# A state-space stage on one core: the block-wise complex recurrence becomes a rotation and one real scan per tile, with its DRAM round trips on another queue and a new order

## The chip, the cores and the metric

The program runs on one core of a Trainium2 chip. TensorE (PE) multiplies matrices, VectorE (DVE) and ScalarE (ACT) work on tiles of 128 partitions, GpSimd (POOL) does some element work, and SP, ACT and POOL issue DMAs. The metric is the device time of one execution in microseconds; lower is better. Runs of the kernel before: 2762.75, 2764.63 and 2765.36 us, median 2764.63.

## What is computed

Two attention blocks, then a second model of two layers; its first layer mixes with a diagonal complex state-space recurrence (64 groups of 16 channels, 64 complex states each, 512 steps). Cut to that mixer:

```python
u = (h @ w_in).reshape(bsz, seq, N_GROUPS, SSM_GROUP)
dt = exp(log_dt)[:, None]
mag = exp(a_re * dt)
ab_re, ab_im = mag * cos(a_im * dt), mag * sin(a_im * dt)
...   # bb = input matrix times (ab - 1) / a
bu_re = einsum('blgh,gph->blgp', u, bb_re)
bu_im = einsum('blgh,gph->blgp', u, bb_im)
# s[t] = ab * s[t-1] + bu[t], complex, along the 512 steps
_, _, s_re, s_im = associative_scan(combine, (ab_re, ab_im, bu_re, bu_im), axis=1)
y = einsum(s_re, c_re) - einsum(s_im, c_im) + d_skip * u
z = gelu(y) @ w_glu
return z[..., :D_MODEL] * sigmoid(z[..., D_MODEL:])
```

## The kernel before

The whole program is one plan of items (`Plan`), each a function with the weight units it needs. `run` walks the items and puts weight DMAs (`raw`, on SP) and weight splits ahead of them: a unit of 128x1024 float32 becomes a high part `wh` (ACT, `emit_split`, L232) and a low part `wl` (DVE, L235), and a wide matmul (128x512) is done as three (high x high, high x low, low x high, `mm3`, L336). Four `wh`/`wl` buffers exist; a split is emitted once fewer than four units are live. Other tiles come from shared rings: `s2` (128x512 float32, 16 of them) and `s4` (twice as wide, 24). PE, DVE and ACT run their instructions in the order that the scheduler of the language fixes; pinned instructions keep the plan's order among themselves.

The state-space stage (`ssm`, L1420) has eight tiles of eight groups. Time is cut into 64 blocks of 8 steps; a block is one column. The operations of the stage have one-letter names in `ORDER`, a hand-written list of plan steps:

- `u i.k`: quarter k of the input matmul of tile i (24 wide matmuls in all). Its evacuation `ev_u` (DVE, L1435) writes `u` to DRAM (`ud`, queue `Q1`) and reads it back in another layout as `U` (queue `Q2`).
- `S i` (`states`): eight 128x64 matmuls with the table `wt` give the state increments of the 64 blocks; ACT copies them from PSUM into `VS`.
- `c k.j` (`scan`): the recurrence over the 64 blocks on DVE, for three parts of two, three and three tiles. Seven `intra` steps inside eight sub-blocks, seven `inter` steps across them (five small operations each, L1472 to L1476, complex times the powers `SR`, `SI`), a `turn` on ACT and one `fix` per tile (three operations, L1498 to L1500) that makes the correction `fx`.
- `T i` (`lags`): eight 128x64 matmuls of `U` with the table `tt`, the part inside a block. `O i` (`outs`): eight matmuls with `VS` and eight with `fx`, both with the table `ot`, added to T's PSUM tile.
- `G i`, `H i`: gelu (ACT, DVE, ACT, DVE); H writes it to DRAM (`yd`, `Q3`) and reads it back (`yT`, `Q4`). `Y i` splits it into high and low.
- `g k`: step k of the first four tiles of the last matmul (`w_glu`), 12 wide matmuls. Later tiles follow as usual.
- `w i` loads `wt` and `tt` of a tile, `o i` loads `ot`; loads are on SP. The first four tiles' `wt`, `tt` are loaded before the stage.

The tables themselves are computed by `ssm_gen` (L1211) as background steps spread evenly through the second ffn1 layer's matmuls: `load`, `mag`, `angle`, `factor`, `inner`, `tables`, `outer` once (small operations on 128x64 and powers by doubling, `powers`, L1271), then per tile `fetch`, `bbar`, `stacks`, the `expansion` of `go`, `lags`, the `expansion` of `gw`, `spread` and `flip`, with results in DRAM (`od`, `gg`, `td`, `wd`).

Before the change `Q1` and `Q3` are ACT's queue, `Q2` and `Q4` SP's.

Of the kernel before, what the change touches and what calls it, by code (L numbers as in the profile page):

```python
# [20 lines left out]
SSM_PARTS = ((0, 2), (2, 5), (5, 8))  # L21
# [32 lines left out]
for _name, _w in (("ident", 128), ("ones_d", 128), ("ones_q", 128), ("ones_kv", 128), ("blk", 128),  # L54
# [53 lines left out]
class Kernel:  # L108
# [21 lines left out]
    LAG = 3  # L130
    W1 = 32
# [13 lines left out]
    def __init__(self, tc, ins, out, upto=None, skip1=False):  # L145
# [9 lines left out]
        self.hold = []  # L155
        self.raw = {}
# [89 lines left out]
    def run(self):  # L246
# [8 lines left out]
        nsplit = ndma = 3  # L255

# [954 lines left out]
    def ssm_gen(self):  # L1211
# [27 lines left out]
        def angle():  # L1239
# [7 lines left out]
            v.tensor_tensor(I[:, 1], g["mag"], sn, ALU.mult)  # L1247

# [48 lines left out]
        def outer():  # L1297

            R, I = [self.s4("gp", F32, [128, 16, 64]) for _ in range(2)]
            v.tensor_copy(R[:, 1], g["R"][:, 8])  # L1300
            v.tensor_copy(I[:, 1], g["I"][:, 8])
            for n in (1, 2, 4):
                powers(R, I, n)
            self.SR = self.apool.tile([128, 64, 8], F32, name="SR")
            self.SI = self.apool.tile([128, 64, 8], F32, name="SI")
            f = lambda x: x[:, 1:9].rearrange("p k g -> p g k")
            nc.gpsimd.tensor_copy(self.SR, f(R))
# [795 lines left out]
```

## Time and profile before

| | |
|---|---|
| median of 3 runs | 2764.63 us |
| the profiled execution: device time | 2768.0 us |
| its span, first to last instruction | 2766.2 us |
| busy: PE, DVE, ACT, POOL | 98%, 67%, 47%, 10% |
| mean granted TensorE clock | 0.987 |
| the stage, `u3` to the end of the written order | 1533.11 to 1679.36 us of the span |

The page cuts the span into 40 slices of 69 us. PE is at 9 tenths or more in all but the first, the last and the two in which the stage lies, where it is at 8; the granted clock shows 8 and 7 tenths in these two. [...] A wait is idle time of an engine, put down to what ended it.

### The profile page before, as it was taken

To read this page: it belongs to the slowest core of one execution; us is meant where nothing else is said; L and a number is where in the kernel's file an instruction comes from. 1 tells how busy PE (TensorE), PEld (TensorE's weight loads), DVE (VectorE), ACT (ScalarE), POOL (GpSimd) and SP (SyncE) were. 2 spreads that over 40 slices of the span, in tenths; PEclk is the share of its full clock that TensorE was granted. 3 is DMA by queue.
4 is the path that set the end of the run, shared out by engine and by line. 5 is a ranking of instruction groups with operands and counts; after the bars stand their busy time and mean duration, and the time that the engine had idled before them with its cause. 6 is when DMAs were issued, how large, how long until landed. Compare 5 with 4: busy or idle time off the path is not lost.

```text
span 2766.2 us, 35309 instructions
## 1 busy us (share of the span) xinstructions
PE 2701.0 (98%) x13466; PEld 2269.5 (82%) x13466; DVE 1842.4 (67%) x2981; ACT 1305.2 (47%) x2208; POOL 273.2 (10%) x287
## 2 busy tenths in 40 slices
PE   8999999999999999999999889999999999999998
PEld 6888888888878888888888788888887888888887
DVE  7889864444687997797745785556456777575554
ACT  5566554332466674633334224433236889542323
POOL 1000000000210100021002000101111111110101
PEclk9999999999999999999999879999999999999999
DMA  5323333233222324354444623333324223233321
GB/s 207 117 71 95 126 117 105 93 98 99 91 104 98 94 85 162 122 191 150 142 124 171 189 90 109 98 99 99 93 85 143 81 84 110 91 94 98 99 93 60
DMA packets 122651, 309.56 MB, mean 112 GB/s; under 512 B 35825, under 2 KB 42737, under 8 KB 122353
## 3 DMA queue, kind: packets, MB, share of 16 engines
q1 hardware_dynamic: 109424, 291.57, 32.8%
q0 software_dynamic: 2432, 7.34, 1.2%
q10 hardware_dynamic: 10624, 8.39, 1.0%
q8 instruction: 106, 1.74, 0.3%
q14 instruction: 65, 0.52, 0.1%
HBM read 260.59 MB, written 41.68 MB: 109 GB/s over the span
## 4 chain that ended last, share of the span: by engine, by line
PE 53%; ACT 5%; DVE 4%; issue 1%; DMA 1%; POOL 1%; SPq 0%; DVEq 0%; POOLq 0%; ACTq 0%
PE mm L314 48%; PE yps L314 2%; PE o L314 1%; DVE wl L235 1%; PE z L314 1%; PE s L314 1%; ACT e L1719 1%; PE vps L314 1%; ACT e L1723 0%; ACT e L1718 0%; ACT sp L358 0%; ACT whl L358 0%; ACT w L1739 0%; PE gps L314 0%; ACT wh L232 0%
## 5 line engine op out<-in xcount | busy, mean ns | idle before, releaser
L314 PE MATMUL mm<-xg,wh 128*128 128x512 f32 (+1 forms) x4080 | 1221.0, 382 | 22.5 <-DVE xg L362 11.6
L314 PEld LDWEIGHTS mm<-xg,wh 128*128 128x128 f32 x4080 | 748.0, 189 | 174.4 <-DVE xg L362 17.4
L232 ACT ACTIVATE wh<-raw 128x1024 fp32r<-128x1024 f32 (+2 forms) x417 | 431.5, 1039 | 823.0 <-PE mm L314 543.8
L314 PE MATMUL mm<-xg,wl 128*128 128x512 f32 (+1 forms) x2024 | 763.0, 379 | 0.0
L235 DVE TENSOR_TENSOR wl<-raw,wh 128x1024 fp32r<-128x1024 f32 (+2 forms) x417 | 529.5, 1273 | 159.3 <-ACT wh L232 157.6
L314 PE MATMUL mm<-hid,wh 128*128 128x512 f32 (+1 forms) x1816 | 539.0, 380 | 0.7 <-DVE hid L359 0.4
L314 PEld LDWEIGHTS mm<-xg,wl 128*128 128x128 f32 x2024 | 382.7, 189 | 71.6 <-issue 0.2
L314 PEld LDWEIGHTS mm<-hid,wh 128*128 128x128 f32 x1816 | 335.0, 188 | 67.0 <-DVE hid L359 1.2
L314 PE MATMUL mm<-hid,wl 128*128 128x512 f32 (+1 forms) x908 | 343.8, 379 | 0.0
L314 PE MATMUL mm<-yhl,wh 128*128 128x512 f32 x640 | 207.6, 403 | 8.7 <-ACT yhl L1539 4.8
L314 PEld LDWEIGHTS mm<-hid,wl 128*128 128x128 f32 x908 | 170.8, 188 | 31.9
L416 POOL TENSOR_TENSOR acc<-acc,sq 128x512 f32<-128x512 f32 (+1 forms) x70 | 89.3, 1275 | 958.2 <-ACT sq L404 845.8
L314 PEld LDWEIGHTS mm<-yhl,wh 128*128 128x128 f32 x640 | 120.7, 193 | 34.6 <-DVE yhl L1540 5.7
L1627 POOL TENSOR_TENSOR gt<-gt,cv 128x512 f32<-128x512 f32 x44 | 78.6, 1787 | 588.2 <-ACT wh L232 452.2
L314 PE MATMUL mm<-yhl,wl 128*128 128x512 f32 x320 | 127.5, 398 | 0.0
L636 DVE SCALAR_TENSOR_TENSOR ht<-mm,rr 128x512 f32<-128x512 f32 x64 | 44.0, 689 | 111.7 <-PE mm L314 111.5
L1635 DVE SCALAR_TENSOR_TENSOR xr<-mm,xr 128x512 f32<-128x512 f32 (+1 forms) x50 | 33.5, 670 | 125.4 <-PE mm L314 125.4
L652 DVE TENSOR_TENSOR part<-part,mm 128x512 f32<-128x512 f32 (+1 forms) x52 | 33.5, 644 | 113.9 <-PE mm L314 113.9
L1615 DVE SCALAR_TENSOR_TENSOR gt<-mm,rr 128x512 f32<-128x512 f32 x88 | 60.4, 689 | 66.2 <-PE mm L314 66.1
L767 DVE TENSOR_REDUCE nm<-s 128x1 f32<-128x512 f32 x128 | 86.4, 680 | 21.9 <-PE s L314 21.5
L794 ACT ACTIVATE pt<-pT 128x512 fp32r<-128x512 f32 x128 | 74.6, 594 | 46.3 <-PE pT L330 45.0
L774 ACT ACTIVATE p<-s,nm 128x512 f32<-128x512 f32 x128 | 87.1, 684 | 10.9 <-DVE nm L767 8.9
(302 smaller groups left out, 3440.5 us busy)
## 6 DMA issues: line engine op xcount, KB each, us to landing
raw<-in_w_up SPq DMA_DIRECT2D x152, 512.0 KB, 3.6
raw<-in_w_down SPq DMA_DIRECT2D x96, 512.0 KB, 3.5
raw<-in_w_in SPq DMA_DIRECT2D x51, 512.0 KB, 3.6
xd<-xr SPq DMA_DIRECT2D x16, 512.0 KB, 3.1
gd<-z SPq DMA_DIRECT2D x32, 256.0 KB, 2.1
g<-gd SPq DMA_DIRECT2D x32, 256.0 KB, 3.9
raw<-in_w_o SPq DMA_DIRECT2D x16, 512.0 KB, 3.6
raw<-in_w_glu SPq DMA_DIRECT2D x16, 512.0 KB, 3.8
```

Of the source, the lines that this page charges most:

```text
L232: ins = self.nc.scalar.activation(h, x, AF.Copy)
L235: ins = lo_engine.tensor_tensor(l, x, h.bitcast(F32), ALU.subtract)
L314: return self.nc.tensor.matmul(out, lhsT, rhs, **kw)
L416: eng.tensor_tensor(st["acc"][:, cols], st["acc"][:, cols], sq[:, cols], ALU.add)
L636: nc.vector.scalar_tensor_tensor(t, ps, 0.0, st["r"], op0=ALU.max, op1=ALU.mult)
L652: nc.vector.tensor_tensor(p, p, ps[:, cols], ALU.add)
L767: nc.vector.tensor_reduce(nm, ps, AX.X, ALU.max, negate=True)
L774: nc.scalar.activation(p, ps, AF.Exp, bias=nm, accum_out=sm)
L794: nc.scalar.activation(hi[:, :, q0:q0 + 128], v, AF.Copy)
L1615: v.scalar_tensor_tensor(t, ps, -0.5, st["r"], op0=ALU.mult, op1=ALU.mult)
L1627: nc.gpsimd.tensor_tensor(t, t, sg.pop(n), ALU.mult)
L1635: v.scalar_tensor_tensor(x, ps[:, cols], 0.5, x, op0=ALU.mult, op1=ALU.add)
```

## The change

The recurrence s[t] = ab s[t-1] + v[t] is turned into a real one: with p the unit phase of a block step and m8 its magnitude, z[c] = conj(p)^c v[c] obeys a recurrence with the real factor m8, which one `tensor_tensor_scan` runs along all 64 blocks of all eight groups of a tile (a zero factor in each group's first column restarts it); turned back by p^c it gives the two operands of O. The phase tables p^c for c = 0 to 63 are made in the background (`turns`, two `wheel`s of eight powers each, and per tile two `table` steps of three operations), written to DRAM (`cd`) and loaded per tile as `tab` (step `b`).

- S leaves its result in PSUM; ACT copies its halves crosswise (`vx`). R (`rotate`): ACT fills the factor tile `m`, DVE does three operations. C (`chain`): the scan, then two crosswise half copies on ACT with a sign. Z (`turn`): two operations on DVE. O: eight matmuls with each of Z's two products.
- `VS`, `SR`, `SI`, `fx`, the three parts and all `c` steps are gone; `outer` becomes `turns` and the wheels.
- `Q1` to `Q4` are GpSimd's queue.
- A split counts a unit as live until three plan items after its last use, within the written order (`SLAG`).
- `w` loads `wt` only, a new step `x` loads `tt`; a new `ORDER`, one tile after another. In the background, `gw`'s expansion comes ahead of `lags`, `flip` ahead of `spread`.

```diff
-SSM_PARTS = ((0, 2), (2, 5), (5, 8))
 ORDER = """
-    u5.0 u5.1 S0 S1 u5.2 c0.0 w5 u5.3 c0.1 u6.0 c0.2 u6.1 c0.3 c0.4 w6 c0.5 c0.6 c0.7 u6.2 c0.8 w4 S2 c0.9 c0.10 w7
...
-    c2.12 c2.13 c2.14 c2.15 c2.16 O5 c2.17 O6 Y4 G5 H5 O7 G6 H6 g3 G7 H7 Y5 g4 g5 Y6 g6 Y7 g7
+    b0 b1 b2 b3 o0 o1 u5.0 u5.1 u5.2 u5.3 S0 u6.0 R0 w4 S1 C0 u6.1 R1 w5 S2 Z0 C1 u6.2 R2 w6 S3 Z1 C2 u6.3 R3 w7 T0 O0 Z2 C3 x4 b4 G0 S4 Z3
+    H0 o2 u7.0 T1 O1 R4 b5 G1 u7.1 x5 C4 H1 o3 u7.2 S5 u7.3 Z4 R5 T2 O2 C5 b6 G2 x6 S6 Z5 H2 o4 R6 Y0 g0 T3 O3 C6 b7 G3 x7 S7 Z6 H3 o5 R7
+    Y1 g1 T4 O4 C7 G4 H4 o6 Z7 T5 O5 Y2 G5 H5 o7 g2 T6 O6 G6 H6 Y3 T7 O7 G7 H7 g3 Y4 g4 Y5 g5 Y6 g6 Y7 g7
 """
-    Q1 = 'scalar'
-    Q2 = 'sync'
-    Q3 = 'scalar'
-    Q4 = 'sync'
+    Q1 = 'gpsimd'
+    Q2 = 'gpsimd'
+    Q3 = 'gpsimd'
+    Q4 = 'gpsimd'
+    SLAG = 3
...
+        seen = seq[:3]
-            live = sum(1 for u in self.whl if last[u] >= i and u not in self.alt)
+            lag = next((n for a, b, n in self.lazy if a <= i < b), 0)
+            live = sum(1 for u in seen if last[u] >= i - lag and u not in self.alt)
...
+        def turns():
+            pr, pi = g["pr"], g["pi"]
+            m8 = self.m8 = self.apool.tile([128, 64], F32, name="m8")
+            v.tensor_tensor(m8, g["mag"], g["mag"], ALU.mult)
+            x, y = T("g_th", [64]), T("g_t", [64])
+            for k in range(3):
+                v.tensor_tensor(x, pr, pr, ALU.mult)
+                v.tensor_tensor(y, pi, pi, ALU.mult)
+                v.scalar_tensor_tensor(pi, pr, 2.0, pi, op0=ALU.mult, op1=ALU.mult)
+                v.tensor_tensor(pr, x, y, ALU.subtract)
+                if k:
+                    v.tensor_tensor(m8, m8, m8, ALU.mult)
+        def wheel(name):
+            def f():
+                R, I = [self.s4("gp", F32, [128, 16, 64]) for _ in range(2)]
...
+                for n in (1, 2, 4):
+                    powers(R, I, n)
+                for z, x in (("r", R), ("i", I)):
+                    t = g[name + z] = self.s2("wh" + z, F32, [128, 8, 64])
+                    nc.gpsimd.tensor_copy(t, x[:, 0:8])
+                    nc.gpsimd.tensor_copy(g["p" + z], x[:, 8])
+            return f
-        ops += [load, mag, angle, factor, inner, tables, outer]
+        ops += [load, mag, angle, factor, inner, tables, turns, wheel("lo"), wheel("hi")]
+        def table(i):
...
+            def part(k, a, b, op):
+                def f():
+                    if k == 0:
+                        box["t"] = self.s4("gt", F32)
...
+                    v.tensor_tensor(o, H("r"), L(a), ALU.mult)
+                    v.tensor_tensor(x, H("i"), L(b), ALU.mult)
+                    v.tensor_tensor(box["t"][:, k], box["t"][:, k], w, op)
+                    if k == 1:
+                        nc.sync.dma_start(self.Cd[i], box["t"])
...
         def states(i):
-            self.pin(nc.scalar.copy(VS[k][:, 8 * (i - a):8 * (i - a) + 8], ps))
+            f = ps.rearrange("p g c -> p (g c)")
+            x = self.s2("vx")
+            self.pin(nc.scalar.activation(x[up], f[dn], AF.Copy))
+            self.pin(nc.scalar.activation(x[dn], f[up], AF.Copy))
+            vp[i] = f, x
+        def load_tab(i):
...
+            tab[i] = self.vpool.tile([128, 2, 512], F32, name="tab", tag="tab", bufs=4)
+            nc.sync.dma_start(tab[i], self.Cd[i])
-        def scan(k):
...
+        def rotate(i):
+            f, x = vp.pop(i)
+            m = ms[i % 2]
+            self.pin(nc.scalar.activation(m[:, :, 1:64], self.m8[:, 8 * i:8 * i + 8].unsqueeze(2).to_broadcast([128, 8, 63]), AF.Copy))
+            t = self.s2("vt")
+            self.pin(v.tensor_tensor(t, f, tab[i][:, 0], ALU.mult))
+            self.pin(v.tensor_tensor(x, x, tab[i][:, 1], ALU.mult))
+            self.pin(v.tensor_tensor(t, t, x, ALU.add))
+            zs[i] = t, m
+        def chain(i):
+            t, m = zs[i]
+            z = self.s2("vz")
+            self.pin(v.tensor_tensor_scan(z, m.rearrange("p g c -> p (g c)"), t, 0.0, ALU.mult, ALU.add))
+            y = self.s2("zx")
+            self.pin(nc.scalar.activation(y[up], z[dn], AF.Copy, scale=-1.0))
+            self.pin(nc.scalar.activation(y[dn], z[up], AF.Copy, scale=-1.0))
+            zs[i] = z, y
+        def turn(i):
+            z, y = zs[i]
+            c = tab.pop(i)
+            self.pin(v.tensor_tensor(z, z, c[:, 0], ALU.mult))
+            self.pin(v.tensor_tensor(y, y, c[:, 1], ALU.mult))
         def outs(i):
+            for x in zs.pop(i):
+                x = x.rearrange("p (g c) -> p g c", g=8)
+                for g in range(8):
+                    self.pin(self.mm(ps[:, g, 1:64], ot[i][:, g], x[:, g, 0:63], start=False, stop=True, skip_group_check=True))
...
+        self.lazy.append((len(P.items), len(P.items) + len(order), self.SLAG))
```

## Rows read from the trace of the kernel before

**Rows 1.** The page's first part: busy time of each engine, share of the span, instructions.
```profile
PE 2701.0 (98%) x13466; PEld 2269.5 (82%) x13466; DVE 1842.4 (67%) x2981; ACT 1305.2 (47%) x2208; POOL 273.2 (10%) x287
```
**Rows 2.** Windows: length, PE, PEld, DVE, ACT, POOL busy (instructions); clock, DMA share, GB/s.
```profile
1533.11:1679.36 146.25, 131.72 (x726) 117.75 (x725) 110.27 (x275) 31.64 (x50) 0.00 (x0) 0.81 0.42 126
1577.46:1614.66 37.20, 34.15 (x160) 34.15 (x161) 33.91 (x94) 7.88 (x12) 0.00 (x0) 0.53 0.49 149
1637.59:1654.35 16.76, 9.22 (x24) 6.02 (x24) 15.68 (x52) 1.15 (x2) 0.00 (x0) 0.69 0.24 71
```
**Rows 3.** Timeline of PE in the stage: start, length, engine, line, operation, tiles, count.
```profile
1540.36 0.62 PE L314 MATMUL mm<-xg,wh 128*128 128x512 f32 x2
...
1541.04 0.62 PE L314 MATMUL mm<-xg,wh 128*128 128x512 f32 x2
...
1560.48 1.89 PE L314 MATMUL vps<-U,wt 128*128 128x64 f32 x16
1562.18 0.71 PE L314 MATMUL mm<-xg,wh 128*128 128x512 f32 x2
...
1583.98 3.62 PE L314 MATMUL vps<-U,wt 128*128 128x64 f32 x16
```
**Rows 4.** Waits of PE in the stage: us in total, times, longest.
```profile
PE mm L314 <- ACT yhl L1539: 4.8, 2, 2.8
PE yps L314 <- DVE VS L1476: 4.1, 2, 3.1
```
**Rows 5.** Windows of the stage, instructions on VS alone, then on fx (no POOL column).
```profile
1533.11:1679.36 146.25, 19.09 (x128) 18.21 (x128) 69.93 (x218) 7.53 (x14) 0.81 0.42 126
...
1533.11:1679.36 146.25, 18.70 (x128) 18.42 (x128) 12.55 (x24) 0.81 0.42 126
```
**Rows 6.** Instructions by tile: wide and small DVE operations, ACT half copies; ns min/median/max.
```profile
L1324 DVE TENSOR_TENSOR go<-g_c,g_P x16: 673/683/686, 1204.4 to 1391.0; 128x512 f32<-128x512 f32 x16
...
L1276 DVE TENSOR_TENSOR g_w<-gp x6: 208/280/413, 1193.2 to 1209.3; 128x64 f32<-128x64 f32 x2, 128x128 f32<-128x128 f32 x2, 128x256 f32<-128x256 f32 x2
...
L1682 ACT ACTIVATE kd<-z x16: 613/629/636, 2125.9 to 2300.2; 64x512 fp32r<-64x512 f32 x16
```
**Rows 7.** Timeline of DVE: the first evacuation of a u tile.
```profile
1537.27 1.13 DVE L1435 SCALAR_TENSOR_TENSOR u<-mm,rr 128x512 f32<-128x512 f32 x1
```
**Rows 8.** DMA issues of the round trips: queue, count, KB each, median us to landing.
```profile
ud<-u ACTq DMA_DIRECT2D x8, 256.0 KB, 4.2
U<-ud SPq DMA_DIRECT2D x8, 256.0 KB, 2.8
yd<-gq ACTq DMA_DIRECT2D x8, 256.0 KB, 2.1
yT<-yd SPq DMA_DIRECT2D x8, 256.0 KB, 2.9
```
**Rows 9.** Instructions by line on GpSimd: 64-row DMA, its landing, 32-row DMA, a copy.
```profile
L1684 POOL DMA_DIRECT2D kd<-kd x16: 509/516/617, 2127.9 to 2301.9; - x16
...
DMA to landing us min/median/max: 2.9/3.9/7.5
...
L1002 POOL DMA_DIRECT2D qh<-qrhl x16: 492/496/768, 218.2 to 1008.3; - x16
...
L1362 POOL COPY g_bs<-g_bb x8: 288/425/2932, 1197.4 to 1362.0; 64x128 f32<-64x128 f32 x8
```
**Rows 10.** Windows of a GpSimd DMA beside DVE, and of the background steps, two halves.
```profile
1000.00:1020.00 20.00, 20.00 (x124) 17.60 (x123) 19.04 (x40) 13.84 (x30) 0.49 (x1) 1.00 0.20 60
...
1180.00:1300.00 120.00, 120.00 (x641) 98.89 (x640) 101.72 (x246) 39.12 (x55) 24.45 (x28) 1.00 0.54 175
1300.00:1420.00 120.00, 120.00 (x647) 98.69 (x646) 74.80 (x118) 36.55 (x51) 6.02 (x12) 1.00 0.46 144
```

More of the change, by code (lines that the diff above doesn't have):

```diff
@@ L155, in __init__ @@
         self.hold = []
+        self.lazy = []
         self.raw = {}
@@ L1295, in tables @@
             v.tensor_scalar(P2[up], I[up], -1.0, None, ALU.mult)
[L1297 to L1307, printed above, removed]
-            nc.gpsimd.tensor_copy(self.SI[up], f(I)[up])
-            v.tensor_scalar(self.SI[dn], f(I)[dn], -1.0, None, ALU.mult)
@@ L1423, in ssm @@
         res = {"xs": [], "st": {}}
-        us, VS, yp, ys = {}, {}, {}, {}
-        HS, FX = {}, {}
-        wt, tt, ot = self.wt, self.tt, {}
+        us, vp, zs, yp, ys = {}, {}, {}, {}, {}
+        wt, tt, ot, tab = self.wt, self.tt, {}, {}
         yT = {}
-        part = {i: k for k, (a, b) in enumerate(SSM_PARTS) for i in range(a, b)}
+        up, dn = slice(0, 64), slice(64, 128)
         def pre():
@@ L1441, in states @@
         def states(i):
-            k = part[i]
-            a, b = SSM_PARTS[k]
-            if i == a:
-                VS[k] = self.vpool.tile([128, 8 * (b - a), 64], F32, name=f"VS{k}")
             ps = self.ps("vps", [128, 8, 64])
@@ L1509, in outs @@
+        def turn(i):
[3 more added lines that the diff above has]
+            self.pin(v.tensor_tensor(y, y, c[:, 1], ALU.mult))
         def outs(i):
-            k = part[i]
-            a = SSM_PARTS[k][0]
             ps = yp[i]
-            for g in range(8):
-                self.pin(self.mm(ps[:, g, 1:64], ot[i][:, g], VS[k][:, 8 * (i - a) + g, 0:63],
-                                 start=False, stop=True, skip_group_check=True))
@@ L1516, in outs @@
-            fx = FX.pop(i, None)
-            for g in range(8 if fx is not None else 0):
-                self.pin(self.mm(ps.rearrange("p g (b k) -> p g b k", b=8)[:, g, 1:8, 1:8], ot[i][:, g], fx[:, g],
-                                 start=False, stop=True, skip_group_check=True))
+            for x in zs.pop(i):
+                x = x.rearrange("p (g c) -> p g c", g=8)
+                for g in range(8):
+                    self.pin(self.mm(ps[:, g, 1:64], ot[i][:, g], x[:, g, 0:63], start=False, stop=True, skip_group_check=True))
@@ L1577, in ssm @@
         for nm, f in (("S", states), ("T", lags), ("O", outs), ("G", gelu), ("H", gelu2), ("Y", ysplit), ("o", load_o),
-                      ("w", self.load_ops)):
+                      ("w", self.load_w), ("x", self.load_t), ("b", load_tab), ("R", rotate), ("C", chain), ("Z", turn)):
             for i in range(8):
                 ops[f"{nm}{i}"] = (lambda f=f, i=i: f(i)), ()
-        for k in range(len(SSM_PARTS)):
-            for j, f in enumerate(scan(k)):
-                ops[f"c{k}.{j}"] = f, ()
         for k in range(KT):
@@ L1881, in build @@
             self.Td = [dt(f"td{i}", [128, 8, 128]) for i in range(8)]
+            self.Cd = [dt(f"cd{i}", [128, 2, 512]) for i in range(8)]
             self.wt, self.tt = {}, {}
```

83 lines of the change are left out of this document (33 added, 50 removed).

## The prediction, made before the changed kernel was built

> **What bounds the kernel now.** I read the page first: PE is busy in 98% of the span [rows 1], so time can only be won where PE stands still or runs slowly. The page's slices show one such place, the state-space stage, where PE falls to 8 tenths, and its clock to 8 and then 7. [...] GpSimd does nothing in it (0.00).
>
> What would the stage's matmuls cost at the full clock? Three 128x512 matmuls take 0.68 us, start to start; the sixteen records of one 128x64 batch (an S step) take 1.70 [rows 3]. The stage has five `u` tiles of 24 wide matmuls (8 groups of three, 5.44 each: 27.2), eight S batches, eight T, sixteen for the O steps (the second half of each is a little narrower now, full width after; both priced as S), that is 32 x 1.70 = 54.4, and eight `g` steps of 12 wide matmuls (2.72 each: 21.8). The sum is 103.4. So 42.9 of the 146.25 us are lost: 14.5 idle, 28.4 to the clock. The waits name the cause: PE stood for `VS` (the recurrence on DVE) and for `yhl`, which the recurrence delays [rows 4]. After the wait before 1580 the clock stayed low for the stretch to 1614.66 (mean 0.53, one S batch 3.62 instead of 1.89) [rows 2, 3].
>
> **The recurrence on DVE.** Removed: 210 small operations on `VS` and 24 on `fx`, 69.9 us and the 16 `fx` operations that do not read `VS`, two thirds of 12.55, 8.4: 78.3 us of DVE [rows 5], in chains as long as a part (three tiles). Added per tile: five 128x512 tensor_tensor, 0.683 each [rows 6], and one scan. [...] Per tile 4.8, for eight 38: DVE in the stage falls from 110 us to about 70, and no chain is longer than a tile. [...]
>
> Chain of one tile, S to O: two half-tile copies on ACT (0.63 each), three operations, scan, two copies, two operations: 1.26 + 2.05 + 1.37 + 1.26 + 1.37 = 7.3 us [rows 6]. ACT gains about 3.1 us a tile (four half copies and the fill of the multiplier tile) less the 0.6 us copy it had; at 31.6 busy of 146 [rows 2] it carries 52 easily. PE's number of matmuls is unchanged: the second eight of each O now read the other product instead of `fx`.
>
> **The round trips.** `u` goes to DRAM and back in another layout, and so does the gelu output. Now ACT issues the writes and SP the reads; landing takes 4.2, 2.8, 2.1 and 2.9 us [rows 8]. After, all four are on GpSimd. It is idle here, so what queues behind a waiting read is only the next trip. Two of the four have 128 rows of 2 KB, the other two 1024 pieces of 256 B. GpSimd's DMAs in this trace have 32 rows (median 496 ns) or 64 (516) [rows 9]. From the two, 0.63 ns a row: 0.56 for 128 rows, 1.1 for 1024 (an estimate). If the whole time went with the rows it would be 8.3 for 1024. I take 1.1, since 32 more rows added only 20 ns. Landing I take as now; the 64-row DMAs landed in 2.9 to 7.5.
>
> A `u` trip then holds GpSimd 1.1 + 4.2 + 0.56 = 5.9 us, a gelu trip 0.56 + 2.1 + 1.1 = 3.8. The first evacuation ends 5.3 us after the stage's start [rows 7]; `U0` is back at 5.3 + 5.9 + 2.8 = 14.0, each next one 5.9 later: 19.9, 25.8, 31.7. In the new order PE reaches S0 at 16.3, S1 at 19.4, S2 at 22.5: S2 and S3 wait about 3 us each. From S4 on PE arrives later than `U`, since T, O and the rest of `u6` and `u7` lie between. O7 ends; gelu (2 x 0.63 + 2 x 0.68), the trip (6.7) and the split (1.3) make 10.6; four `g` steps (10.9) cover it. So idle time is 6 us by this walk; 2 if the reads leave in another order than written; 18 if the trips before `g0` and `g1` each queue behind a whole `u` trip (5.9). I take 8.
>
> The clock follows the waits. In 1637.59 to 1654.35, two waits before wide matmuls, it cost (1 - 0.69) x 9.22 = 2.9, 1.4 a wait; in 1577.46 to 1614.66, a wait before narrow batches only, (1 - 0.53) x 34.15 = 16 [rows 2]. For three or four waits I take 8, half the long case, with ends 2 and 20. The new stage: 103.4 + 8 + 8 = 119.4, 26.8 less.
>
> [...]
>
> **Weight splits that lag.** Splits come three plan items (about 4 us) later. Today a split emitted before its buffer is free holds DVE in front of a `u` evacuation; that goes. Price: nothing, as four weight buffers hold 21.8 us of PE work and a unit is still forced in before first use. If that cover failed, PE would wait for a split, two operations of double width on ACT and DVE, 2.6 us [rows 6], once per unit, for nine units 23.
>
> **Tables, loads and SP.** Under ffn1's matmuls DVE gains 16 x 3 x 0.683 = 32.8 for the tables, 18 x 0.28 = 5.0 for the second wheel, 16 x 0.21 = 3.4 for the turns [rows 6]: 41 us. There DVE is busy 101.7 and 74.8 of two stretches of 120, PE 120 of 120 [rows 10]. About 23 of the 41 fall in the first: 125 of 120, so preparation slips some 5 us, into the second half, which has 27 free. PE's own needs of DVE come first in the written order, so I take 2, between 0 and 5. SP gets eight 512 KB table writes and eight reads, and loses 16 reads that waited for writes; the first four table reads and two `ot` loads, moved to the front, share the DMA engines at 0.42 busy in the mean [rows 2]. T loads are split off W loads and come later, after S3 frees `wt`. I price these at nothing; if they came late, R0 would wait for `tab`.
>
> **Rivals.**
> *GpSimd binds (slower).* Sixteen trips in one queue hold it 16p + 8 x 4.8 + 8 x 2.7 = 16p + 60, with p the cost of a 1024-piece issue; with the start (5.3) and the tail (2.9 + 1.3 + 2.7) the stage is 16p + 72. It passes 146 from p = 4.6. At 5.5, two thirds of the proportional 8.3, it is 160: 2780. [...]
> *The clock eats it.* PE waits once inside the narrow batches and stays low to the last O: idle 14, clock 20, stage 137: 9 less, 2758. For it: the stretch to 1614.66 now; against it: `g` steps, wide, stand between the late batches.
> *Preparation stalls PE.* The 41 us do not fit, or four `s2` buffers held by the wheels block an evacuation: each time PE loses one tile's matmuls, 5.4, three times 16 in all, 2754. For it: DVE at 101.7 of 120; against it: PE at 120 of 120 there.
> *Almost no waits.* Trips leave out of order: 103.4 + 2 + 2, 39 less, and nothing for preparation: 2726.
>
> **How the numbers follow.** The sum is made against the profiled execution, 2768.0 us; the median shown is 3.4 below it. 2768.0 - 26.8 + 2 - 3.4 = 2739.8, so 2740. Chances: forecast 0.55 (2731 to 2750), clock 0.14, GpSimd 0.11, preparation 0.08, almost no waits 0.12. The range takes in the best bounds (2726) and the worst idle and clock (18 and 20: 141.4, 4.9 less) with 4 for preparation (2768.0 - 4.9 + 4 - 3.4 = 2764); only the GpSimd rival lies outside. A measurement of this kernel can tell about 0.2%, 5.5 us, from no change: faster is below 2759, which holds the forecast, the best case, most of the clock and preparation cases: 0.82; same 0.08, slower 0.10.
>
> **What would show it.** Right: stage length near 119, DVE about 70 there, no PE wait on a DVE chain, POOL DMA issues near 0.6 and 1.1 us. Wrong: POOL DMA records of several us, S or `yhl` waits over 3 us, a granted clock below 0.85 in the stage, or PE idle between 1180 and 1420.

## The result and the profile after

The changed kernel took 2792.9 us (median of 4 runs, 2790.0 to 2798.5) against 2765.0 for the kernel before in the same session: a ratio of 1.0104, 95% interval 1.0086 to 1.0123. It is slower, and the prediction (2740, range 2726 to 2764) was wrong. The profiled execution took 2791.2 us with a span of 2789.5.

The page's first part, to be read beside [rows 1]: PE's share fell from 98% to 97%, and GpSimd, whose busy time was 273.2 us, now has the round trips as well.

```profile
PE 2695.3 (97%) x13466; PEld 2260.8 (81%) x13466; DVE 1844.5 (66%) x2884; ACT 1322.7 (47%) x2234; POOL 318.5 (11%) x327
```

To compare kernels I cut at two events that all of them have: the start of the last mean matmul (the stage's start) and of the first tanh of a gate (its end). I call the stretch from 1180 us to the stage's start the preparation; up to about 1180 us the traces of the two kernels are equal. Windows of the kernel before, cut so (columns as in [rows 2]):

```profile
1180.00:1532.66 352.66, 345.32 (x1843) 287.78 (x1842) 240.80 (x459) 123.22 (x189) 50.16 (x57) 1.00 0.49 158
1532.66:1679.36 146.70, 132.17 (x727) 117.97 (x726) 110.72 (x275) 32.09 (x50) 0.00 (x0) 0.81 0.42 126
```

and of the changed one:

```profile
1180.00:1551.48 371.48, 352.46 (x1847) 290.69 (x1846) 284.89 (x549) 124.79 (x191) 73.72 (x65) 0.98 0.51 168
1551.48:1704.08 152.60, 121.36 (x727) 108.48 (x726) 67.98 (x89) 48.59 (x75) 23.36 (x32) 0.83 0.41 135
```

So two stretches lost time. The preparation (first line) grew by 18.8 us: PE idle 19.0 in place of 7.3 (length minus PE busy), and 7.1 more busy, which is lower clock (0.98 in place of 1.00). The stage grew by 5.9: DVE fell from 110.7 to 68.0 as forecast, but PE stood still 31.2 us in place of 14.5. With 1.4 us less behind the stage this is the 23.3 us between the two spans. (The medians lie 27.9 apart, since the profiled execution of the kernel before is 3.4 us above its median and that of the changed one 1.7 below.)

PE's waits in the changed kernel's preparation (us in total, times, longest). The two shown are at the lag products, which write the tile `gps`; they are 10.5 us, where the kernel before has none:

```profile
PE gps L316 <- POOL g_bs L1408: 6.5, 2, 5.1
PE gps L316 <- DVE go L1374: 4.0, 1, 4.0
```

and in its stage:

```profile
PE mm L316 <- ACT yhl L1569: 21.0, 2, 18.3
PE yps L316 <- DVE vz L1541: 6.3, 1, 6.3
PE mm L316 <- DVE yhl L1570: 2.1, 1, 2.1
PE vps L316 <- DMA U<-ud: 1.8, 1, 1.8
```

So in the preparation PE waits for a small copy on GpSimd and for an addition on DVE. In the stage it waits for the first output block's operand (`yhl`) and for tile 0's states (`vz`); nobody waits for the recurrence as a chain any more [rows 4].

**Who stands ahead on ACT.** The timeline of ACT in the stage (start, length, ..., idle before it and its releaser):

```profile
1568.68 1.06 ACT L231 ACTIVATE wh<-raw 128x1024 fp32r<-128x1024 f32 x1 [4.38 <-PE mm L316]
1586.63 1.06 ACT L231 ACTIVATE wh<-raw 128x1024 fp32r<-128x1024 f32 x1 [16.89 <-PE mm L316]
1587.71 0.59 ACT L1496 ACTIVATE vx<-vps 64x512 f32<-64x512 f32 x1
...
1609.94 0.60 ACT L1554 ACTIVATE gq<-yps 128x512 f32<-128x512 f32 x1 [1.97 <-PE yps L316]
1619.27 1.06 ACT L231 ACTIVATE wh<-raw 128x1024 fp32r<-128x1024 f32 x1 [8.73 <-PE mm L316]
1620.35 1.28 ACT L336 ACT_TABLE_LOAD   x1
1621.64 0.63 ACT L336 ACTIVATE gq<-gq 128x512 f32<-128x512 f32 x1
```

S0's matmuls on PE:

```profile
1568.71 1.89 PE L316 MATMUL vps<-U,wt 128*128 128x64 f32 x16
```

They were done near 1570.5, but its copies `vx` stand behind a weight split that needs a buffer which `u6`'s last matmul frees at 1586.6. In the plan the split is written far later (behind O0; in e2, below, it runs there); since it is not pinned, it stands ahead of S0's copies in ACT's order. A second split stands the same way ahead of tile 0's tanh.

**Why the lag products were late.** The changed kernel's timeline at 1420 us, on GpSimd:

```profile
1420.26 6.24 POOL L1407 COPY g_bs<-g_bb 64x128 f32<-64x128 f32 x1 [8.35 <-DVE g_bb L1400]
```

on DVE, the first and the last of ten operations:

```profile
1420.25 0.69 DVE L1370 TENSOR_TENSOR cx<-g_c,g_P 128x512 f32<-128x512 f32 x1
...
1425.66 0.69 DVE L1370 TENSOR_TENSOR cx<-g_bb,g_P 128x512 f32<-128x512 f32 x1
```

and on PE:

```profile
1426.91 0.29 PE L316 MATMUL gps<-g_c,g_bs 128*32 128x16 f32 x2 [5.08 <-POOL g_bs L1408]
```

DVE ran ten wide operations without a gap from 1420.25 to 1426.35, and the copy, 0.28 us at its shortest, began with the first and ended (1426.50) behind the last. PE, in order, stood for it, and the window from 1420 to 1432, which holds the wait and what came after it, has a granted clock of 0.72.

**Prices that came out.** GpSimd's transfers and the scan in the stage (line, operation, count, busy us, mean ns, idle before):

```profile
L1485 POOL DMA_DIRECT2D ud<-u x8 | 7.3, 919 | 21.9 <-DVE u L1483 21.7 <-issue 0.2
L1564 POOL DMA_DIRECT2D yT<-yd x8 | 7.2, 901 | 27.0 <-issue 8.8 <-DMA yd<-gq 8.6 <-ACT m L1522 7.1
L1487 POOL DMA_DIRECT2D U<-ud x8 | 4.4, 551 | 31.6 <-DMA ud<-u 15.0 <-issue 6.6 <-ACT zx L1535 5.6
L1532 DVE TENSOR_TENSOR_SCAN vz<-m,vt 128x512 f32<-128x512 f32 x8 | 9.8, 1222 | 1.3 <-DMA yd<-gq 1.1
```

### The profile page after: what moved, and what is told of

It reads as the page before. It is cut to its first block, busy times and chain, and to the rows that moved or that the text cites. A ratio compares the mean times of both kernels' runs of the same rounds, so it can differ in the third digit from the quotient of the medians.

```text
span 2789.5 us, 35328 instructions
## 1 busy us (share of the span) xinstructions
PE 2695.3 (97%) x13466; PEld 2260.8 (81%) x13466; DVE 1844.5 (66%) x2884; ACT 1322.7 (47%) x2234; POOL 318.5 (11%) x327
## 4 chain that ended last, share of the span: by engine, by line
PE 49%; DVE 6%; ACT 5%; issue 2%; DMA 1%; POOL 1%; SPq 0%; DVEq 0%; POOLq 0%; ACTq 0%
PE mm L316 44%; PE yps L316 1%; DVE wl L234 1%; ACT wh L231 1%; PE s L316 1%; ACT e L1747 1%; PE o L316 1%; ACT e L1746 1%; ACT e L1751 1%; ACT sp L360 0%; ACT whl L360 0%; ACT w L1767 0%; PE gps L316 0%; DVE e L1752 0%; PE z L316 0%
```

## The experiments

S is the start of the stage, L its length to the first gate, idle is L less PE's busy time, clock is the mean granted clock in L; these four are of the one profiled execution. The second column is the median of 4 to 10 executions, and the ratio is to the kernel before, with its 95% interval.

| run | us | ratio | S | L | idle | clock |
|---|---|---|---|---|---|---|
| before | 2763.7 to 2765.9 | 1 | 1532.7 | 146.7 | 14.5 | 0.81 |
| changed | 2792.9 | 1.0104 [1.0086, 1.0123] | 1551.5 | 152.6 | 31.2 | 0.83 |
| e1 queues back | 2782.2 | 1.0069 [1.0054, 1.0084] | 1550.2 | 143.5 | 24.8 | 0.87 |
| e2 splits pinned | 2774.7 | 1.0044 [1.0021, 1.0068] | 1549.3 | 136.5 | 22.5 | 0.90 |
| e10 both | 2765.5 | 1.0004 [0.9993, 1.0014] | 1549.5 | 126.6 | 15.6 | 0.93 |
| e11 pinned, stores GpSimd, loads SP | 2764.3 | 0.9992 [0.9981, 1.0003] | 1549.5 | 132.1 | 14.7 | 0.87 |
| e5 six buffers | 2787.8 | 1.0085 [1.0068, 1.0102] | 1548.6 | 151.9 | 30.0 | 0.83 |
| e6 e2 + e5 | 2779.4 | 1.0047 [1.0032, 1.0062] | 1549.6 | 141.7 | 19.9 | 0.84 |
| e14 e10 + e5 | 2766.0 | 1.0002 [0.9988, 1.0016] | 1551.6 | 131.5 | 13.8 | 0.87 |
| e9 e2, g later | 2793.5 | 1.0095 [1.0075, 1.0114] | 1550.9 | 156.1 | 30.4 | 0.81 |
| e3 copies on DVE | 2791.2 | 1.0099 [1.0084, 1.0114] | 1546.6 | 155.2 | 31.8 | 0.82 |
| e4 lags early | 2789.1 | 1.0102 [1.0083, 1.0120] | 1549.7 | 151.2 | 33.0 | 0.85 |
| e7 e3, lags behind table | 2790.4 | 1.0093 [1.0076, 1.0110] | 1548.3 | 153.8 | 32.0 | 0.83 |
| e8 one table | 2785.1 | 1.0073 [1.0058, 1.0088] | 1543.2 | 155.2 | 31.4 | 0.82 |
| e12 begun earlier | 2795.2 | 1.0098 [1.0077, 1.0120] | 1551.5 | 153.6 | 32.6 | 0.83 |
| e13 e10 + e3, lags 30 later | 2750.2 | 0.9942 [0.9921, 0.9963] | 1533.0 | 127.4 | 15.0 | 0.92 |
| e15 same, 60 later | 2753.6 | 0.9960 [0.9946, 0.9975] | 1537.1 | 127.4 | 15.0 | 0.92 |
| e18 e13 without e3 | 2753.5 | 0.9955 [0.9940, 0.9970] | 1536.9 | 127.7 | 15.3 | 0.92 |
| e16 e13, gelu first | 2755.6 | 0.9959 [0.9944, 0.9974] | 1534.4 | 134.1 | 15.4 | 0.86 |
| e17 e16, y first | 2750.2 | 0.9943 [0.9929, 0.9957] | 1533.7 | 126.8 | 14.8 | 0.93 |

S moved by up to 3 us between kernels whose preparation is the same (1548.6 to 1551.6), and L by about as much where only the preparation differs (151.2 to 155.2): smaller differences decide nothing. Executions of one kernel also differ, and the mean clock with them: e10's ten took 2764.0 to 2772.0 us at 0.992 to 0.988. The profiled execution lay within 2 us of its kernel's median but for the kernel before (3.4 above), e11 (4.3 above) and e14 (5.5 above); the S, L and clock of these say less than their medians.

### The stage: order on ACT, or GpSimd's queue

e1, the queues alone back (`Q1` to `Q4`):

```diff
-    Q1 = 'gpsimd'
-    Q2 = 'gpsimd'
-    Q3 = 'gpsimd'
-    Q4 = 'gpsimd'
+    Q1 = 'scalar'
+    Q2 = 'sync'
+    Q3 = 'scalar'
+    Q4 = 'sync'
```

> The changed kernel with one part undone: the four transfers of a tile's two round trips go out from ACT and SP again instead of GpSimd. In the changed kernel's trace the stage runs from its mean matmul at 1551.65 us to the last output block's matmuls near 1699 (147 us), and GpSimd's queue holds a tile's issue behind the one before it (second ud at 1562.24, though u was ready at about 1558; yT of tile 0 issued 1630.91, 7.6 us after yd). If that queue is what ate the gain (the prediction's first rival), the stage falls to about 125 us and the run to about 2770. If the stage is held by ACT's order (two weight splits wait 16.9 and 8.7 us for a matmul with the copies of tile 0 behind them), the stage stays within 5 us of 147, or grows, since ACT then issues two transfers of each tile behind the same splits. The preparation before the stage has no round trips: mean matmul within 1.5 us of 1551.65 by either.

(The texts of e1 to e4 count the stage to 1699, some 5 us before my end: 147 there is 152.6 here.) L fell by 9.1 us, between what the two theories expected: GpSimd's queue costs, but holds only part.

e2, the splits of the stage pinned (`lag` is 3 in the stage, 0 elsewhere; `...` is the condition that was there):

```diff
-self.emit_split(u, any(...))
+self.emit_split(u, lag > 0 or any(...))
```

> The changed kernel with one edit: in the stage the weight splits on ACT and VectorE are kept in program order, as the stage's other instructions are, so that the split written after step O0 is no longer ahead of S0's copies on ACT. Theory ACT order: the waits of 16.9 us (1569.7 to 1586.6) and 8.7 us (1610.5 to 1619.3) go; PE's waits of 6.3 us for tile 0's states and a good part of the 18.3 us for tile 0's split output go with them, and the clock they cost: the stage 147 to about 125 us (range 118 to 134), the run about 2769. Rival, the ring of 16 half-buffers: waits for a free buffer (scan, vt, u, gq, U and yT waited 1 to 7 us each) take the place, and the stage stays above 140. The preparation is untouched: mean matmul within 1.5 us of 1551.65.

L fell by 16.1 us, and the wait for `vz` went. The window and PE's waits of e2:

```profile
1549.26:1685.78 136.52, 114.05 (x726) 100.92 (x725) 68.07 (x89) 49.67 (x76) 23.36 (x32) 0.90 0.44 151
```

and

```profile
PE mm L316 <- ACT yhl L1569: 16.1, 3, 12.6
PE vps L316 <- issue: 3.6, 2, 3.2
PE mm L316 <- DVE yhl L1570: 2.8, 2, 2.6
```

By the count of the text the stage is about 131 us, within the first theory's range (118 to 134) and far from the ring's "above 140", but 6 us over its 125: 12.6 us at `g0` stayed.

e10, both edits:

> Weight splits in program order, and the four transfers of a tile issued by ACT and SP as in the kernel before. Queues alone took the stage from 152.6 to 143.5, the order of the splits alone to 136.5. If GpSimd's one queue is a bound of its own (U and yT waited there 15 and 10 us for transfers ahead of them), both together give about 128 (range 123 to 132). If the splits' place was what the other queues also relieved, 136 +- 3.

26.0 us less, as the first theory expected; alone they gave 9.1 and 16.1, which add up to 25.2, so they are two separate causes. The medians agree: 10.7, 18.2 and together 27.4 us less than the changed kernel. e10's window and PE's waits in it:

```profile
1549.49:1676.12 126.63, 111.00 (x727) 99.84 (x726) 68.13 (x89) 49.98 (x77) 0.00 (x0) 0.93 0.52 162
```

and

```profile
PE mm L316 <- ACT yhl L1569: 14.5, 3, 10.5
PE mm L316 <- DVE yhl L1570: 1.2, 1, 1.2
```

e11, stores on GpSimd and loads on SP (`Q2` and `Q4` to `'sync'`, splits pinned):

> Weight splits in program order; the two stores of a tile (ud, yd) on GpSimd and the two loads (U, yT), which wait for the stores to land, on SP. Of the same question as the run with ACT and SP: if what costs is a store standing behind a load that waits for its own store to land, this frees it without giving ACT any issue, and the stage falls to about 126 (range 121 to 131); if SP's own loads of weights and factors stand ahead of the trips, or the queue was never the bound, 134 or more.

PE idle fell to e10's level, 14.7. L, 132.1, lies between e2 and e10, but it is of an execution 4.3 us above the median; by the medians e11 is as fast as e10 (2764.3 and 2765.5). So stores issued by GpSimd cost nothing that shows. What cost the time is the one queue, in which a load that waits for its own store to land holds the next store: in the changed kernel GpSimd stood 15.0 us ahead of the loads `U` and 8.6 ahead of `yT` for a store to land (the lines under "Prices that came out"). Other ways to divide the four transfers were not tried.

### The stage: the ring of half-buffers

e5, six buffers a tile in place of eight (`x` is the swapped copy, handed on from `rotate`):

```diff
-            zs[i] = t, m
+            zs[i] = t, m, x
...
-            t, m = zs[i]
-            z = self.s2("vz")
+            t, m, y = zs[i]
+            z = t
...
-            y = self.s2("zx")
```

> The changed kernel with fewer tiles from the ring of 16 half-buffers: the scan writes over its input and the two negated copies write over the first rotation's second product, so that a tile takes 6 buffers of the ring (u, U, vt, vx, gq, yT) and not 8, with the same instructions in the same order of steps. Stage of the changed kernel: 152.6 us from its last mean matmul (1551.48) to the first gate (1704.08), of the kernel before 146.7. Theory ring: in the changed kernel buffers, not data, hold the scan, u of tile 7 (2.4 us), gq (2.0, 2.4), U (5.6, 4.4) and yT (7.1) back; these waits go and the stage falls to about 138 (range 132 to 143). Theory ACT order: the weight splits still stand ahead of S0's copies, and the stage stays within 5 us of 152.6. The time before the stage is untouched.

e6 has it with the splits pinned:

> The two edits together: weight splits in program order in the stage (alone: 152.6 to 136.5 us) and 6 buffers of the ring a tile. If the ring is what holds the stage once the splits are in order (in that run ACT's negated copy waited 10.8 us for a transfer's buffer, gq of tile 2 3.1, and U of tile 6 6.8), the stage falls to about 124 (range 118 to 130). If it is GpSimd's queue (the same waits are then for the transfer itself, which stands behind two round trips of y), the stage stays within 4 us of 136.5.

and e14 with the queues apart as well:

> The run with splits in order and ACT's and SP's queues (stage 126.6 us, PE idle 15.6 of it, 10.5 at g0), and 6 buffers of the ring a tile in place of 8. On GpSimd's queue the smaller need made no gain (141.7 against 136.5). If the ring is what holds tile 0's output back once the queues are apart, the wait at g0 falls from 10.5 to 5 or less and the stage to about 120 (range 117 to 123). If it is not a bound, 126.6 +- 3.

The ring fell as a cause three times: none of the gains that it promised came. e5 lies 5.1 us under the changed kernel in its median, with overlapping intervals, but only 0.7 in L, where the ring would act. PE idle shrank by 1.3, 2.6 and 1.9 us, and L did not follow: in the profiled executions of e6 and e14 PE was busy 7.7 and 6.7 us longer, at a clock of 0.84 against 0.90 and 0.87 against 0.93. In e14 that is no effect of the buffers: its executions took 2765.1 us at a mean clock of 0.992 as well as the profiled 2771.5 at 0.988, and its median is e10's. In e6 the medians do differ (2779.4 and 2774.7), but its fastest execution, 2773.1, equals e2's, so whether six buffers cost anything is open. e6's window:

```profile
1549.59:1691.24 141.65, 121.75 (x727) 108.99 (x726) 67.93 (x89) 49.78 (x76) 23.34 (x32) 0.84 0.42 145
```

### The stage: the wait at g0

e9, `Y0 g0` to `Y3 g3` one tile later, splits pinned:

```diff
-R6 Y0 g0 T3 O3 C6 b7 G3 x7 S7 Z6 H3 o5 R7 Y1 g1 T4 ...
+R6 T3 O3 C6 b7 G3 x7 S7 Z6 H3 o5 R7 Y0 g0 T4 ... Z7 Y1 g1 T5 ...
```

> Weight splits in program order, and besides the first four blocks of the output projection one tile later in the written order: Y0 g0 behind S7 Z6 H3 R7 in place of ahead of T3 O3, Y1 g1 behind Z7, Y2 g2 ahead of T6, Y3 g3 ahead of T7. With the splits in order alone, PE waited 12.6 us at g0 for tile 0's split output (O0's last batch began at 1588.3, g0 at 1624.5: 36 us, where the prediction had reckoned 10.6 from an output batch to its g), with T3, O3 and S7 behind it. Theory, PE's order puts g0 ahead of its data: the wait goes, T3, O3 and S7 fill it, the stage falls from 136.5 to about 125 us (range 120 to 130). Rival, the chain through ACT, GpSimd's queue and the ring is itself late: the wait moves to the next matmuls in line (O3, g1, or the last g's), and the stage stays above 132.

My theory fell: S7 now waited for its round trip, `g0` still waited, and four later `g` steps 2.6 us each. Two of e9's lines on PE's timeline:

```profile
1625.37 3.65 PE L316 MATMUL vps<-U,wt 128*128 128x64 f32 x16 [5.55 <-DMA U<-ud]
1637.96 2.08 PE L316 MATMUL mm<-yhl,wh 128*128 128x512 f32 x4 [8.94 <-ACT yhl L1569]
```

With the queues apart and the preparation mended (e13, below) I tried ACT's place for the gelu and for the split of its output instead:

```diff
-T0 O0 Z2 C3 x4 b4 G0 S4 ...      # e16, and so for G1 to G4
+T0 O0 G0 Z2 C3 x4 b4 S4 ...
-H2 o4 R6 Y0 g0                   # e17, and so for Y1 g1
+H2 o4 Y0 g0 R6
```

> The run with splits in order, ACT's and SP's queues and the lags 30 matmuls later (2750.2 us, stage 132.7, PE waits 9.9 us at g0), and besides the gelu of tiles 0 to 4 right behind its output batch in the written order (G0 ahead of Z2 C3, G1 ahead of R4, G2 ahead of C5, G3 ahead of C6, G4 ahead of C7). In that run O0's matmuls ended at 1568.2 and ACT came to tile 0's square at 1577.2, behind the negated copies of tile 3, which waited 3.7 us for its scan, and a weight split. Theory, ACT's order holds tile 0's output: the square comes at about 1570, all of tile 0's trip 6 to 7 us earlier, the wait at g0 falls to 3 or 4 and the stage to about 125 (range 121 to 129), the run to about 2743. Rival, the trip is late at its other end (ACT's split copy of y stood at 1599.2 behind tile 5's gelu and tile 6's copies): wait and stage stay within 2 us.

> The run before and besides Y0 g0 ahead of R6 and Y1 g1 ahead of R7, so that ACT splits tile 0's output before tile 6's swapped copies. Theory, the trip is held at its other end: the split copy of y comes when its data have landed, some 3 us earlier, and the wait at g0 falls below 3 us; stage 2 to 4 us under the run before. Rival, ACT now waits for the trip with tile 6's copies behind it, and S7's chain is later by the same: within 2 us of the run before, or worse.

(The 132.7 in the text of e16 was read to the second gate; to the first it is 127.4.) Neither moved the wait by much: 9.2 and 8.7 us at `g0`, against 9.9. In e17 the wait at `g1` grew besides, from 3.0 to 5.1. In e16 the stage was even longer, at the same idle time, by the clock; its window:

```profile
1534.42:1668.53 134.11, 118.68 (x727) 107.14 (x726) 68.06 (x89) 49.76 (x76) 0.00 (x0) 0.86 0.49 153
```

The traces show where the time went. At the near end e16 and e17 gained nothing: ACT's first gelu operation came 39.2 us after S in place of 44.3, but tile 0's store `yd` was issued 46.8 us after S in both, against 47.6 in e13. Its last operation on DVE is part of `H0`, which still stood behind `Z3`. At the far end, in e17, the load of tile 0 was issued at 1587.54 and landed 3.9 us later, at 1591.4; ACT came to split it at 1598.77:

```profile
1591.73 0.58 ACT L1554 ACTIVATE gq<-yps 128x512 f32<-128x512 f32 x1
1594.04 0.63 ACT L336 ACTIVATE gq<-gq 128x512 f32<-128x512 f32 x1 [1.74 <-DVE gq L1555]
...
1598.40 0.33 ACTq L1562 DMA_DIRECT2D yd<-gq  x1
1598.77 0.63 ACT L1569 ACTIVATE yhl<-yT 128x512 fp32r<-128x512 f32 x1 [1.11 <-DVE gq L1561]
```

These are tile 2's gelu and store, with the copies of tiles 5 and 6 between: the steps `G2 C5 S6 H2`, which the order writes ahead of `Y0` in e17 as well. So some 7 of the 8.7 us at `g0` are again ACT's order, now the written one, to which pinned instructions are held. No run moved `Y0` ahead of `G2`, so what that would win, and what it would cost tile 2, is not shown.

### The preparation: load, list, or PE's order

e3 moved the copies of `g_bs` and of the wheels to DVE:

```diff
-                    nc.gpsimd.tensor_copy(t, x[:, 0:8])
-                    nc.gpsimd.tensor_copy(g["p" + z], x[:, 8])
+                    v.tensor_copy(t, x[:, 0:8])
+                    v.tensor_copy(g["p" + z], x[:, 8])
...
-                nc.gpsimd.tensor_copy(bs[up], bb[up, 0])
-                nc.gpsimd.tensor_copy(bs[dn], bb[dn, 1])
+                v.tensor_copy(bs[up], bb[up, 0])
+                v.tensor_copy(bs[dn], bb[dn, 1])
```

> The changed kernel with the preparation's copies of the lag stack (g_bs, two a tile) and of the two wheels moved from GpSimd to VectorE, which runs just ahead of them anyway. In the changed kernel's trace the copy of 64x128 took 0.28 us when VectorE was idle or on small work and 6.24 us from 1420.26, ending as VectorE's run of 128x512 operations ended; PE waited 5.1 us for it there and 1.5 at 1335, and the wheel's 128x512 copy took 9.30 us against 0.95 to 1.5. Theory GpSimd starved by VectorE: those two PE waits vanish and the clock dip after the second (0.72) with them, the mean matmul moves from 1551.65 to about 1543 (range 1541 to 1546), the run to about 2782. Rival, VectorE's own backlog: VectorE gets 16 copies of about 0.2 us and 8 bigger ones more, the PE waits move from GpSimd's copy to VectorE's adds and the mean matmul stays within 2 us of 1551.65 or later. The stage (147 us) is untouched.

PE's waits for GpSimd went, but a wait of 4.5 us came back behind the copy on DVE (at 1390), and 2.8 at the wheels stayed: 5 us won, not 8.5.

e4 and e12 moved the work in the list: `[lags]` ahead of the second expansion; `BG = 60` to `BG = 40`.

> The changed kernel with one part of the new order undone: the lag products of each tile again stand before the expansion of the second stack in the background list (as in the kernel before), not behind it. Theory GpSimd starved by VectorE's long runs: with the lags' matmuls 6 operations earlier in the list, the copy they need still ends only with VectorE's run, and PE meets it as early or earlier: PE waits of the 5.1 and 1.5 us kind stay or grow, the mean matmul at 1550 to 1556. Rival, the reorder itself is what lost the time: the waits vanish, mean matmul at about 1540. The stage (147 us) is untouched by either.

> The changed kernel with the preparation begun 20 items of the feed-forward earlier (from item 40, not 60), so that the same operations are spread over a longer stretch; nothing else. With one table in place of eight the start of the stage came from 1551.5 to 1543.2. Theory, the load per time on VectorE: PE's waits of 4.0, 1.5 and 5.1 us get shorter or go, and the stage starts at 1543 or earlier (range 1536 to 1546). Rival, each tile's own burst (two expansions and a table back to back) is what PE's lag products meet, however far apart the tiles are: the start stays within 3 us of 1550. A third: at its earlier place the preparation meets the stretch from 1000 to 1040 where VectorE is busy 38.65 of 40 us, and the loss shows there.

Neither gained. In e12 the 4.0 became 0.5, and GpSimd's copy held PE longer; from e12's waits before the stage:

```profile
PE gps L316 <- POOL g_bs L1408: 8.6, 1, 8.6
```

e7, e3 with `[lags]` behind the table, gave nothing over e3 (1548.3):

> Preparation alone: the copies of the lag stack and of the wheels on VectorE (alone this moved the start of the stage from 1551.5 to 1546.6), and besides the lag products of a tile put behind its table in the list, so that PE is asked for them one table (six operations of 0.7 to 1.15 us) later. Theory: PE's remaining waits (4.5 us at 1390 on VectorE's copy, 2.8 on its add at 1220) are PE's instructions standing in order too close behind VectorE's work; put later they go, and the stage starts at about 1538 (range 1536 to 1542). Rival, VectorE has too much to do in the stretch: the waits only move, and the stage starts at 1546 or later.

e8 left out seven of the eight tables (`if i: return` in `part`, table 0 written to all eight):

> The changed kernel without seven of the eight tiles' rotation tables: only tile 0's is computed and written eight times, and all tiles use it (left out: 42 of 48 wide operations of the preparation on VectorE; its states are so not those of the reference). This measures what the tables cost the preparation. Theory, the load on VectorE: with some 36 us of VectorE's work gone PE's waits at 1335, 1360 to 1385 and 1421 go (1.5, 1.0 and 5.1 us), only the one behind the wheels at 1221 (4.0) stays, and the stage starts at about 1539 (range 1537 to 1543) instead of 1551.5. Rival, the order of the list: the second stack's expansion still stands between the lag stack and the lags, GpSimd's copy is still held while it runs, and the stage starts at 1546 or later. The stage itself within 4 us of 152.6.

e8's preparation:

```profile
1180.00:1543.19 363.19, 348.51 (x1838) 288.68 (x1837) 250.29 (x500) 123.83 (x189) 55.52 (x65) 0.99 0.52 171
```

DVE had 34.6 us less to do and 8.3 of the 18.8 us came back, a result between the two expectations; 10.5 stayed with almost the load of before (250 against 241). So load was not the whole cause, and I tried the other: PE's own order.

e13 (on e10, with e3's copies; `later(30, f)` writes `f` into PE's order 30 wide matmuls later, about 6.8 us), e15 with 60 and 90, e18 as e13 with the copies on GpSimd:

```diff
-... + [lags] + table(i) + [flip, spread]
+... + [lambda: self.later(30, lags)] + table(i)
+    + [lambda: self.later(30, flip), lambda: self.later(60, spread)]
```

> The stage as in the run with splits in order and ACT's and SP's queues (126.6 us, start 1549.5); in the preparation the copies on VectorE, and a tile's lag products and transposes written into PE's order 30 wide matmuls (6.8 us at 0.227 us) later than their place in the list, the stores of the lags' blocks 60. Theory, PE's order: the lags stand so close behind VectorE's adds and copies in PE's order that any lateness of VectorE stops PE, though VectorE has idle time over the stretch (285 of 372 us busy); the waits of 4.0, 5.1 and 1.5 us go and with them the clock that each costs after it, the stage starts at about 1537 (range 1534 to 1541) and the run is at about 2752. Rival, VectorE's load: the waits move to the main matmuls (the products' evacuations and weight splits on VectorE are late) and the stage starts at 1544 or later.

> The same with 60 wide matmuls (13.6 us) for the lag products and transposes, 90 for the stores. Theory, PE's order: whatever wait is left at 30 goes at 60, unless the four large buffers of a tile, held 7 us longer, make the next tile's first operation wait on VectorE with the weight splits behind it; start within 2 us of the run with 30 or up to 3 us earlier. Rival, VectorE's load: no earlier than with 30.

> The run with the lags 30 matmuls later (start of the stage 1533.0, 2750.2 us), but with the copies of the lag stack and the wheels on GpSimd again. It tells which half of that edit won the preparation's loss back. If GpSimd's copies, held while VectorE runs its 128x512 operations (6.24 and 9.30 us in the changed kernel against 0.28 and 0.95 free), were half of the loss, 6.8 us of distance just covers the 6.2 and not the wheel's: PE waits of 2 to 5 us come back at the wheels and the stage starts at 1536 to 1543. If the distance in PE's order is all of it, the start is within 2 us of 1533.

The windows of e13:

```profile
1180.00:1532.96 352.96, 344.04 (x1836) 286.46 (x1835) 286.06 (x564) 121.75 (x187) 46.28 (x41) 1.00 0.53 175
1532.96:1660.32 127.36, 112.36 (x727) 100.69 (x726) 68.16 (x89) 50.01 (x77) 0.00 (x0) 0.92 0.51 162
```

The whole loss of the preparation is gone: 352.96 against 352.66 before, at a DVE load of 286.06, no less than in the changed kernel (284.89). No lag product waits any more; PE's waits in e13's preparation are these:

```profile
PE mm L316 <- DVE xg L364: 6.5, 9, 2.7
PE mm L316 <- DVE hid L643: 1.4, 2, 1.0
PE mm L316 <- ACT xg L612: 1.1, 2, 0.8
```

e18 shows that the distance alone brings 12.6 of the 16.5 us between e10 and e13, with no wait at a lag product either; e15 shows that more distance adds nothing. The lag products, the transposes (`flip`) and the stores (`spread`) were moved together; that it was the lag products is read from the waits. Whether the last 4 are the copies' engine is open, since e15, with the copies on DVE, also starts at 1537.1. e13 and e17, at 2750.2 us, are faster than the kernel before by 0.6% and than the changed one by 1.5%.

## Why the prediction was wrong

**DVE's part was right.** DVE in the stage was forecast at about 70 and measured at 68.0. The 1.37 us that the sums take for a scan no run shows: it was my estimate, and the changed kernel's scans took 1.22, 1.8 times a tensor_tensor's 0.69. PE no longer waits on a recurrence.

**The round trips: price right, order wrong.** GpSimd's issues took 0.55 and 0.90 us where 0.56 and 1.1 were estimated; the rival "GpSimd binds" needed 4.6 and did not happen. Its 5.5 us for an issue no run shows: the longest `ud` issue was 1.01, in a stage with DVE busy 68.0 us of 152.6. Yet the queue cost 9 to 10 us (e1, e2 to e10). The walk through it did count loads that hold the next store, for S0 to S3; there PE waited 1.8 us in place of 6. It took queueing trips before `g0` and `g1` only as its bad end, 18 us of idle time; with the queues back (e1) the wait at `g0` alone fell from 18.3 to 12.8.

**The step from O to g failed in place, not in kind.** I priced 10.6 us and covered it with four `g` steps at the end. But `g0` stands in the middle: in the changed kernel O0's last batch began at 1598.3 and `g0` at 1644.9, and in e13 it was 33 us still (1566.4 to 1599.8). "I take 8" of idle time became 31.2; e10 has 15.6. The terms of the 10.6 for tile 0, in e17's trace: from O0's end to the store 11.4 us, where the gelu alone was priced at 2.6; the store's landing 7.0 in place of 2.1; the load's 3.9 in place of 2.9; then the 7.4 behind other tiles' steps on ACT, which the sum did not have.

**"Weight splits that lag. Price: nothing" was the largest error in the stage.** I checked that PE would not lack a split, and gave 23 us if it did. What happened is the reverse: a split that no one yet needs stood ahead of S0's copies on ACT and waited for its buffer. 16.1 us (e2). ACT had the time (48.6 us busy of 152.6), but not the order. The written order was taken for ACT's order, which it is only for pinned instructions. Whether the lag itself or the new step order moved the split there was not separated.

**The clock.** 8 was taken with ends 2 and 20; the changed kernel lost 18.0 (121.4 less 103.4), e10 7.6, e13 9.0. With the two causes undone the size is right, at about twice the idle time that it was taken for, so in part by luck.

**The preparation: load right, consequence wrong.** DVE got 44.1 us (284.89 less 240.80), 41 forecast. The failed sentence is "PE's own needs of DVE come first in the written order, so I take 2". The lag products are themselves PE's needs; they stand in PE's order right behind DVE's and GpSimd's work, so any lateness there stops PE. The sign that the prediction named, PE idle between 1180 and 1420, came: 6.5 us, against none before. The rival "preparation stalls PE" had nearly the size (16) at a chance of 0.08, but by luck: its mechanism was work that does not fit or an evacuation blocked by a held buffer, and of PE's 11.7 us of further idle time 10.5 are at the lag products. With 6.8 us of distance the price of DVE's work is 0.3 (e13) to 4.3 (e18), inside "between 0 and 5".

**Together.** 119.4 was the forecast stage; 126.6 to 127.4 is what the same recurrence, tables and loads give with splits in order, queues apart and the lags later. e13's stage is 19.3 us shorter than before where 26.8 were forecast; its idle time is 15.0 in place of 8, 9.9 of it at `g0`. The preparation costs 0.3 in place of 2. That makes about 6 of the 10 us between 2740 and 2750; the rest lies between the profiled executions and the medians (3.4 us for the kernel before, 1.3 the other way for e13).

## What to carry to other kernels

A written order is an engine's order only where it is fixed; before pricing a step at nothing, look at which waiting instruction may stand ahead of it on each in-order engine. Work that a busy engine does "in the background" costs nothing only if the in-order consumer is kept at a distance from it: here 44 us more on DVE cost 18.8 us of the preparation without distance, and 0.3 to 4.3 with 6.8 us of it. A wait's price is read together with the clock behind it: in e6 2.6 us less idle time came with a stage 5.1 us longer. And a stage's length from one profile is compared only after a look at how far that execution lies from its kernel's median.

## What the hardware showed

GpSimd's copy of 64x128 took 0.28 us at its shortest and 6.24 beside ten adjoining DVE operations, a copy of 128x512 took 0.95 at its shortest and 9.30; both long ones ended within 0.2 us of the end of DVE's gapless run. The second copy, and the last operation of DVE's run beside it:

```profile
1220.29 9.30 POOL L1329 COPY whr<-gp 128x512 f32<-128x512 f32 x1 [6.27 <-DVE gp L1284]
```

```profile
1229.03 0.36 DVE L1430 SCALAR_TENSOR_TENSOR g_gs<-gps,consts,g_gs 128x128 f32<-128x128 f32 x1
```

The copy of 64x128 lasted beyond all ten operations, 0.15 us past the end of the run at 1426.35. What held it is not shown here.

PE idle time and lost clock do not go together in these profiles: e6 stood 2.6 us less than e2 and ran 7.7 longer, e16 stood 0.4 more than e13 and ran 6.3 longer. The clock also differs between executions of one kernel: e14's ten took from 2765.1 us at a mean of 0.992 to 2771.5 at 0.988. What decides it is not shown here.
